# Weight halves at places inside their tiles that differ from load to load

## The chip, the cores and the metric

One Trainium2 chip, of which the kernel uses one core. The metric is the device time of one execution in microseconds (us), from the chip's own clock. The kernel is a single launch; weights come from the chip's memory inside the measured time.

## The reference, cut to what matters

Two transformer blocks of two layers each, in float32, on 512 positions of width 1024. The first block has, per layer, sliding-window attention, a causal depthwise convolution and latent attention side by side, gated and summed, then an MLP with a squared ReLU. The second block carries a second stream of 256 context positions through its first layer; that layer mixes differential attention with a recurrent (delta-rule) mixer, the next one a state-space scan with gated linear attention, and each ends in the same kind of MLP. What the change touches is the plain matrix product that stands in all of them:

```python
x = x + jnp.square(jax.nn.relu(h @ w_up[l])) @ w_down[l]          # first block, two layers
def _sq_relu_mlp(h, w1, w2):
    return jnp.square(jax.nn.relu(h @ w1)) @ w2                   # second block, two layers
```

## The kernel before, in words

Activations stand transposed in SBUF: 128 channels on the partitions, 512 positions (256 for the context stream) along the free axis. A product of a weight block of 1024x128 with the activations is eight steps of contraction, each on a 128x128 piece of the weights.

TensorE multiplies float32 here in a form that keeps fewer bits (fp32r), so every operand is split into a high part (the value cast to fp32r) and a low part (what the cast left out). `load_w` (from L211) does this for weights: SyncE brings a block of 128x1024 float32 into the tile `raw` (L222), ScalarE casts it into `whi` (L223) and VectorE writes the rest into `wlo` (L224). `split` (from L198) does the same for activations, into `hi` and `lo`. `mm3` (from L227) makes three matmuls of one step: `whi` with `hi` (L230), `whi` with `lo` (L231) and `wlo` with `hi` (L232). The weights are the stationary operand, loaded into the array once for each matmul (the rows of engine PEld), the activations the moving one. So one block costs 24 matmuls with 512 moving columns, and 24 more with 256 where the context stream runs along.

`weights(parts)` opens a pool for the weight tiles. Each of `raw`, `whi` and `wlo` has its buffers side by side, two of `raw` and `parts` of the other two, taken in turn by successive loads. `parts` is 2 nearly everywhere, 3 for a pool of the second block's first output projection (`out_proj`), and 4 for the last layer's MLP, which also does half of that layer's output projection. Every weight tile is 1024 float32 long, 4096 bytes on each partition, and its data begin at its first byte. Loads run ahead of their use: a load can start as soon as the buffer's last reader is done.

Where the tiles lie is decided when the program is built. Taken modulo 256 bytes (all weight buffers of one pool give the same number, since 4096 is a multiple of 256; so do the activations of one stage) the first bytes are, as the program is laid out:

| stage | moving tiles (`hi`, `lo`) | `whi`, `wlo` | difference |
|---|---|---|---|
| first block, all products (the two MLPs fill 400 to 870 us and 1210 to 1690 us) | 224 | 224 | 0 |
| second block, `out_proj`, output chunks 0 to 2 (weights from the pool of 3) | 64 | 64 | 0 |
| second block, `out_proj`, later chunks (weights from the pool of 2 on the other side) | 64 | 224 | 160 back, or 96 on |
| second block, first layer's MLP (to about 3115 us), both streams | 160 | 224 | 64 |
| second block, last layer's MLP (about 3580 to 3885 us) | 224 | 224 | 0 |

Other operands lie at places of their own. The convolution's taps (L638) read `u[:, j:j + T]` with j from 1 to 30, 4 bytes further at each tap. `conv` in `odd_features` writes `raw[:, 262:774]` (L1846), 1048 bytes into its tile. The weights of L1439 are a slice of a packed tile of constants that begins 40 bytes past a multiple of 64.

The order of the work is written out by hand: generators that `weave` advances in turn, one instruction stream per engine. The change moves nothing in it.

Of the kernel before, what the change touches and what calls it, by code (L numbers as in the profile page):

```python
# [20 lines left out]
P = 128  # L21
# [6 lines left out]
class Build:  # L28
    def __init__(self, tc, ctx, A, out, dbg=None):
        self.tc, self.nc, self.ctx, self.A, self.out = tc, tc.nc, ctx, A, out  # L30
        self.dbg = dbg or {}
        self.uid = 0
        self.phases, self.psp = [], []


# [174 lines left out]

    def load_w(self, src, kc, cols=P):  # L211
        nc = self.nc
        def t(tag, dt, bufs):
            w = self.wp.tile([P, 1024], dt, tag=tag, name=self.nm(tag), bufs=bufs)
            return w[:, :kc * cols].rearrange("p (k m) -> p k m", k=kc)
        raw, hi, lo = t("raw", F32, 2), t("whi", F32R, self.wparts), t("wlo", F32R, self.wparts)
        if isinstance(src, list):
            for i, one in enumerate(src):
                k = kc // len(src)
                nc.sync.dma_start(out=raw[:, i * k:i * k + k], in_=one.rearrange("p (k m) -> p k m", k=k))  # L220
        else:
            nc.sync.dma_start(out=raw, in_=src)  # L222
        nc.scalar.copy(out=hi, in_=raw)  # L223
        nc.vector.tensor_tensor(out=lo, in0=raw, in1=hi.bitcast(F32), op=ALU.subtract)  # L224
        return hi, lo
# [2288 lines left out]
```

## Time and profile before

| | us |
|---|---|
| median of two runs | 3913.18 |
| lowest and highest | 3912.67, 3913.69 |
| the profiled execution | 3924.51 |
| its span, first to last instruction | 3922.4 |
| mean granted TensorE clock in it | 0.969 of full speed |

The profile page gives each engine's busy time, the chain of work that ended last, and the costliest groups of instructions by line. PE is TensorE's matmuls, PEld its weight loads, DVE VectorE, ACT ScalarE, POOL GpSimd. Matmuls are pipelined: one begins before the one ahead of it has left the array, so the durations of a group add up to more than PE's busy time, and what a matmul costs in a stream is read from one start to the next.

### The profile page before, as it was taken

How to read it: one execution, taken by the hardware profiler on the slowest of the kernel's cores; microseconds unless marked ns; L12 is line 12 of the kernel's file. 1: busy time of each engine (PE TensorE's matmuls, PEld its weight loads, DVE VectorE, ACT ScalarE, POOL GpSimd, SP SyncE). 2: the span in 40 equal slices, each digit the busy share in tenths (PEclk: the TensorE clock that was granted, in tenths of full speed). 3: DMA queues.
4: the chain of work that ended last, by engine and by line, in shares of the span. 5: the costliest groups of instructions: out<-in, count | busy, mean ns of one | idle time of the engine just before them, and what ended most of it. 6: DMA issues, size and time to landing. Idle time of an engine off the chain costs nothing.

```text
span 3922.4 us, 54927 instructions
## 1 busy us (share of the span) xinstructions
PE 3765.1 (96%) x21506; PEld 2966.9 (76%) x21506; DVE 2398.5 (61%) x4178; ACT 1739.6 (44%) x3923; POOL 97.0 (2%) x204
## 2 busy tenths in 40 slices
PE   8999999999999999999998999899999999899998
PEld 5566888886667888778885666788888887678887
DVE  7587567665786566657646667554444574756444
ACT  4655343334553333335537788441222265533332
POOL 0000000000000000000001000000000000000000
PEclk9999999999999999999998989999999999879999
DMA  3132345542132355531110000212112212012232
GB/s 130 49 92 81 100 156 179 158 147 64 57 92 86 118 169 168 192 115 47 45 44 2 2 2 2 82 54 65 65 60 65 83 54 64 6 60 94 97 97 76
DMA packets 115699, 324.98 MB, mean 83 GB/s; under 512 B 12528, under 2 KB 34032, under 8 KB 115440
## 3 DMA queue, kind: packets, MB, share of 16 engines
q1 hardware_dynamic: 115440, 321.47, 25.6%
q8 instruction: 169, 2.77, 0.3%
q14 instruction: 90, 0.74, 0.1%
HBM read 307.27 MB, written 12.58 MB: 82 GB/s over the span
## 4 chain that ended last, share of the span: by engine, by line
PE 78%; issue 11%; ACT 6%; DVE 4%; POOL 1%; DMA 1%; SPq 0%; POOLq 0%; DVEq 0%; ACTq 0%
PE ps_g L230 20%; PE ps_g L232 20%; PE ps_g L231 20%; ACT B L1621 1%; PE ps_mm L1564 1%; PE ps_y L750 1%; PE ps_sc L740 1%; POOL r L308 1%; PE ps_y L825 1%; PE ps_z L1531 1%; PE ps_sc L796 1%; PE ps_g L2161 1%; PE ps_y L1236 1%; PE ps_sc L454 1%; DVE wlo L224 1%
## 5 line engine op out<-in xcount | busy, mean ns | idle before, releaser
L230 PE MATMUL ps_g<-hi,whi 128*128 128x512 f32 (+1 forms) x4464 | 1671.5, 375 | 21.2 <-ACT whi L223 13.6
L232 PE MATMUL ps_g<-hi,wlo 128*128 128x512 f32 (+1 forms) x4464 | 1655.7, 371 | 10.3 <-DVE wlo L224 10.2
L231 PE MATMUL ps_g<-lo,whi 128*128 128x512 f32 (+1 forms) x3744 | 1402.3, 375 | 2.3 <-DVE lo L954 1.8
L223 ACT CAST whi<-raw 128x1024 fp32r<-128x1024 f32 (+3 forms) x497 | 481.7, 970 | 1249.3 <-PE ps_g L231 1068.9
L230 PEld LDWEIGHTS ps_g<-hi,whi 128*128 128x128 f32 x4464 | 847.3, 190 | 190.3 <-ACT whi L223 23.7
L232 PEld LDWEIGHTS ps_g<-hi,wlo 128*128 128x128 f32 x4464 | 846.4, 190 | 167.1 <-DVE wlo L224 17.1
L231 PEld LDWEIGHTS ps_g<-lo,whi 128*128 128x128 f32 x3744 | 711.6, 190 | 135.1 <-issue 10.5
L224 DVE TENSOR_TENSOR wlo<-raw,whi 128x1024 fp32r<-128x1024 f32 (+3 forms) x497 | 557.2, 1122 | 165.2 <-ACT whi L223 159.4
L231 PE MATMUL ps_g<-x,whi 128*128 128x512 f32 (+1 forms) x720 | 252.4, 351 | 0.0
L1130 DVE SCALAR_TENSOR_TENSOR x<-ps_g,mod,x 128x512 f32<-128x512 f32 (+1 forms) x192 | 127.1, 662 | 203.3 <-PE ps_g L232 203.3
L879 DVE SCALAR_TENSOR_TENSOR macc<-mraw,cs,macc 128x1024 f32<-128x1024 f32 x140 | 175.7, 1279 | 7.8 <-DMA mraw<-in_mod_w 7.5
L638 DVE SCALAR_TENSOR_TENSOR cv<-u,taps,cv 128x512 f32<-128x512 f32 x240 | 177.2, 745 | 1.1
L1109 DVE TENSOR_SCALAR r<-ps_g 128x512 f32<-128x512 f32 x96 | 57.6, 602 | 184.1 <-PE ps_g L232 181.2
L231 PEld LDWEIGHTS ps_g<-x,whi 128*128 128x128 f32 x720 | 138.0, 192 | 16.4 <-issue 1.6
L589 DVE TENSOR_TENSOR x<-ps_g,x 128x512 f32<-128x512 f32 x64 | 44.1, 690 | 138.3 <-PE ps_g L232 138.2
L473 DVE TENSOR_TENSOR o<-ps_g,R 128x512 f32<-128x512 f32 x76 | 52.2, 690 | 114.6 <-PE ps_g L232 110.8
L1110 ACT ACTIVATE r<-r 128x512 f32<-128x512 f32 x96 | 53.5, 558 | 145.6 <-DVE r L1109 145.6
L308 POOL TENSOR_TENSOR r<-v,mhalf 128x4 f32<-128x4 f32 (+2 forms) x30 | 38.5, 1284 | 2801.4 <-DVE v L327 2135.6
L582 DVE SCALAR_TENSOR_TENSOR r<-ps_g,R 128x512 f32<-128x512 f32 x64 | 44.0, 688 | 81.3 <-PE ps_g L232 77.4
L204 DVE TENSOR_TENSOR lo<-r,hi 128x512 fp32r<-128x512 f32 x96 | 57.7, 601 | 40.7 <-ACT hi L203 40.7
L1621 ACT COPY B<-ps_lv 32x64 f32<-32x64 f32 x384 | 77.5, 202 | 6.3
L291 ACT ACTIVATE sq<-x 128x512 f32<-128x512 f32 (+1 forms) x91 | 49.1, 543 | 70.0 <-DVE x L1130 34.8
(509 smaller groups left out, 4581.1 us busy)
## 6 DMA issues: line engine op xcount, KB each, us to landing
raw<-in_l_mlp_w SPq DMA_DIRECT2D x128, 512.0 KB, 3.4
mraw<-in_mod_w SPq DMA_DIRECT2D x96, 512.0 KB, 4.4
raw<-in_w_in SPq DMA_DIRECT2D x82, 512.0 KB, 3.5
raw<-in_w_up SPq DMA_DIRECT2D x64, 512.0 KB, 3.5
raw<-in_w_down SPq DMA_DIRECT2D x64, 512.0 KB, 3.5
raw<-in_l_w_in SPq DMA_DIRECT2D x50, 512.0 KB, 3.5
raw<-in_w_branch SPq DMA_DIRECT2D x48, 256.0 KB, 2.9
bias<-biasD SPq DMA_DIRECT2D x16, 512.0 KB, 3.9
```

The costliest lines, as they stand in the source:

```text
L204: nc.vector.tensor_tensor(out=lo, in0=src, in1=hi.bitcast(F32), op=ALU.subtract)
L223: nc.scalar.copy(out=hi, in_=raw)
L224: nc.vector.tensor_tensor(out=lo, in0=raw, in1=hi.bitcast(F32), op=ALU.subtract)
L230: t.matmul(ps, w[0], x[0], start=start, stop=False)
L231: t.matmul(ps, w[0], x[1], start=False, stop=False)
L232: t.matmul(ps, w[1], x[0], start=False, stop=stop)
L308: self.nc.gpsimd.tensor_tensor(out=r, in0=v, in1=self.mhalf[:, :v.shape[1]], op=ALU.pow)
L638: nc.vector.scalar_tensor_tensor(out=y, in0=u[:, j:j + T], scalar=taps[:, c * 31 + j:c * 31 + j + 1], in1=y, op0=ALU.mult, op1=ALU.add)
L879: nc.vector.scalar_tensor_tensor(out=acc[s], in0=rw, scalar=self.cs[:, k, s:s + 1], in1=acc[s], op0=ALU.mult, op1=ALU.add)
L1109: nc.vector.tensor_scalar(out=t, in0=ps[s][:, :n], scalar1=0.0, scalar2=None, op0=ALU.max)
L1130: nc.vector.scalar_tensor_tensor(out=xx[c], in0=ps[:, :n], scalar=md[:, s, 5, c:c + 1], in1=xx[c], op0=ALU.mult, op1=ALU.add)
L1621: nc.scalar.copy(out=B[rows, :, j, :], in_=blocks(ps[rows, 0:64]))
```

## The change

`load_w` makes the tiles of `whi` and `wlo` longer by `pad` elements (16, and 128 where the pool has four parts), and lets their data begin at an offset that steps through sixteen values, one at each load: 0 to 15 elements (0 to 60 bytes, by 4), or 0 to 120 elements (0 to 480 bytes, by 32) in the last layer. The high and low parts of one load have the same offset. `raw` stays as it was. No instruction is added, removed or moved.

```diff
-        self.uid = 0
+        self.uid = self.nload = 0
...
     def load_w(self, src, kc, cols=P):
         nc = self.nc
+
+        self.nload += 1
+        pad = 128 if self.wparts == 4 else 16
+
         def t(tag, dt, bufs):
-            w = self.wp.tile([P, 1024], dt, tag=tag, name=self.nm(tag), bufs=bufs)
-            return w[:, :kc * cols].rearrange("p (k m) -> p k m", k=kc)
+            o = 0 if tag == "raw" else self.nload % 16 * (pad // 16)
+            w = self.wp.tile([P, 1024 + (0 if tag == "raw" else pad)], dt, tag=tag, name=self.nm(tag), bufs=bufs)
+            return w[:, o:o + kc * cols].rearrange("p (k m) -> p k m", k=kc)
         raw, hi, lo = t("raw", F32, 2), t("whi", F32R, self.wparts), t("wlo", F32R, self.wparts)
```

## Rows read from the trace of the kernel before

**Rows 1.** The page: busy time by engine, and the chain that ended last.
```profile
PE 3765.1 (96%) x21506; PEld 2966.9 (76%) x21506; DVE 2398.5 (61%) x4178; ACT 1739.6 (44%) x3923; POOL 97.0 (2%) x204
...
PE 78%; issue 11%; ACT 6%; DVE 4%; POOL 1%; DMA 1%; SPq 0%; POOLq 0%; DVEq 0%; ACTq 0%
```

**Rows 2.** Groups by line and shape: count, busy us, mean ns, idle before and releasers.
```profile
L230 PE MATMUL ps_g<-hi,whi 128*128 128x512 f32 x3432 | 1374.9, 401 | 18.8 <-ACT whi L223 11.2 <-ACT hi L206 6.9 <-ACT hi L953 0.6
...
L224 DVE TENSOR_TENSOR wlo<-raw,whi 128x1024 fp32r<-128x1024 f32 x417 | 509.8, 1223 | 164.8 <-ACT whi L223 158.9 <-PE ps_r L2073 0.7
L223 ACT CAST whi<-raw 128x1024 fp32r<-128x1024 f32 x417 | 438.2, 1051 | 1177.1 <-PE ps_g L231 1044.9 <-issue 109.1 <-DMA raw<-in_l_w_out 7.0
L230 PE MATMUL ps_g<-hi,whi 128*128 128x256 f32 x1016 | 290.3, 286 | 2.4 <-ACT whi L223 2.4
```

**Rows 3.** Four stretches, matmuls that read wlo alone (one in three): length, busy (count), clock.
```profile
400.00:870.00 470.00, 263.14 (x676) 1.00 0.47 150
...
1210.00:1690.00 480.00, 265.09 (x677) 0.99 0.46 149
...
2520.00:3115.00 595.00, 374.72 (x1108) 1.00 0.20 63
...
3580.00:3885.00 305.00, 174.61 (x449) 1.00 0.31 100
```

**Rows 4.** Timeline of PE, first block's MLP: start us, duration; the second is 24 later.
```profile
499.98 0.39 PE L230 MATMUL ps_g<-hi,whi 128*128 128x512 f32 x1
...
505.42 0.39 PE L230 MATMUL ps_g<-hi,whi 128*128 128x512 f32 x1
```

**Rows 5.** Timeline of PE, last layer's MLP: the second is 24 matmuls later.
```profile
3650.14 0.39 PE L230 MATMUL ps_g<-hi,whi 128*128 128x512 f32 x1
...
3655.58 0.39 PE L230 MATMUL ps_g<-hi,whi 128*128 128x512 f32 x1
```

**Rows 6.** Timeline of PE, out_proj, weights of the pool of 3: twelve matmuls apart.
```profile
2510.99 0.39 PE L232 MATMUL ps_g<-hi,wlo 128*128 128x512 f32 x1
...
2513.71 0.39 PE L232 MATMUL ps_g<-hi,wlo 128*128 128x512 f32 x1
```

**Rows 7.** Timeline of PE, out_proj, weights of the other pool: each 24 matmuls apart.
```profile
2529.23 0.28 PE L230 MATMUL ps_g<-hi,whi 128*128 128x256 f32 x1
...
2532.11 0.39 PE L230 MATMUL ps_g<-hi,whi 128*128 128x512 f32 x1
...
2537.71 0.28 PE L230 MATMUL ps_g<-hi,whi 128*128 128x256 f32 x1
```

**Rows 8.** Timeline of PE, second block's first MLP: each 24 matmuls apart.
```profile
2701.17 0.28 PE L230 MATMUL ps_g<-hi,whi 128*128 128x256 f32 x1
...
2704.00 0.39 PE L230 MATMUL ps_g<-hi,whi 128*128 128x512 f32 x1
...
2709.59 0.28 PE L230 MATMUL ps_g<-hi,whi 128*128 128x256 f32 x1
```

**Rows 9.** Timeline of PE after a break, first block: five matmuls, then three more.
```profile
256.05 0.39 PE L231 MATMUL ps_g<-lo,whi 128*128 128x512 f32 x1
...
257.20 0.39 PE L230 MATMUL ps_g<-hi,whi 128*128 128x512 f32 x1
...
257.88 0.39 PE L230 MATMUL ps_g<-hi,whi 128*128 128x512 f32 x1
```

**Rows 10.** Groups by line and shape: operands at odd places (all but L951).
```profile
L638 DVE SCALAR_TENSOR_TENSOR cv<-u,taps,cv 128x512 f32<-128x512 f32 x240 | 177.2, 745 | 1.1
...
L951 DVE SCALAR_TENSOR_TENSOR t<-x,gs,R 128x512 f32<-128x512 f32 x24 | 17.0, 746 | 4.5 <-ACT R L342 4.5
...
L1846 ACT COPY raw<-ps_g 128x512 f32<-128x512 f32 x8 | 4.7, 582 | 8.3 <-PE ps_g L232 8.3
...
L1439 PEld LDWEIGHTS ps_mm<-feat,cv 64*128 64x128 f32 x48 | 7.6, 185 | 5.0 <-issue 2.9 <-DVE S L1712 0.5 <-DVE Mh L1566 0.3
```

**Rows 11.** Timeline: a weight load and a copy of 128x512 at even places.
```profile
3500.30 0.19 PEld L230 LDWEIGHTS ps_r<-hi,whi 128*128 128x128 f32 x1
...
3511.26 0.59 ACT L342 COPY R<-ps_r 128x512 f32<-128x512 f32 x1 [8.09 <-PE ps_r L339]
```

## The prediction

> **What bounds the kernel now.** I read the page first: engine shares, then the chain. PE is busy for 96% of the span and stands for 78% of the chain that ended last, with 11% more in which PE mostly just issues; VectorE is at 61% and ScalarE at 44% [rows 1]. So this is a kernel bound by TensorE, and a change to the weights matters if it changes what a matmul costs, or if it makes ScalarE or VectorE late with a weight tile. The groups by line and shape say which matmuls count: each of the three lines of `mm3` has some 3432 with 512 moving columns and 1016 with 256, so about 10,300 wide ones and 3,050 narrow ones in all, and they hardly ever wait for a weight tile: 11.2 us in total for `whi` ahead of the wide ones of L230 [rows 2].
>
> What one of them costs is read in the timeline, from start to start, because the durations overlap. In the first block's MLP 24 wide matmuls take 505.42 - 499.98 = 5.44 us, 226.7 ns each [rows 4]. In the last layer's MLP it is 3655.58 - 3650.14 = 5.44 us, the same [rows 5]. In the second block's first MLP it is 2709.59 - 2704.00 = 5.59 us, 232.9 ns [rows 8], though the shape, the engine and the code are the same and the granted clock is 1.00 in this stretch as in the others [rows 3]. That difference is what the prediction is about.
>
> The table of places gives a reason. Where the spacing is 226.7 ns, the moving tiles and the weight tiles begin at the same byte modulo 256; where it is 233 ns they don't. The best evidence is `out_proj`, since there the moving tiles are the same ones throughout and only the pool of the weights changes. With weights at the same place modulo 256, twelve wide matmuls take 2513.71 - 2510.99 = 2.72 us, 226.7 ns each [rows 6]; with weights from the other pool, 160 bytes off, 24 take 2537.71 - 2532.11 = 5.60 us, 233.3 ns each [rows 7]. So the place of the weights relative to the moving operand is worth 6.6 ns of 226.7 on a wide matmul. For narrow ones it is little and of either sign: 2532.11 - 2529.23 = 2.88 us for 24, or 120.0 ns, at a difference of 160 [rows 7], and 2704.00 - 2701.17 = 2.83 us, or 117.9 ns, at a difference of 64 [rows 8].
>
> One more thing is seen where PE was held up: after a break the wide matmuls start at 230 ns (five from 256.05 to 257.20) and come to 226.7 ns only then (three from 257.20 to 257.88) [rows 9]. The low spacing is a rhythm that a run of matmuls falls into, and that only equal places let it keep.
>
> **The change part by part.** *The longer tiles.* 1040 elements are 4160 bytes, 64 more than a multiple of 256; so in a pool of two, the second buffer of `whi` and of `wlo` lies 64 bytes further, modulo 256, than the first. In the last layer 1152 elements are 4608 bytes, a multiple of 256, and all four buffers keep one place. The pools begin lower by a multiple of 256, so the first buffer's base stays where it was. The number of buffers is the same, no wait is added, and no transfer is moved.
>
> *The offsets.* In the pools of two and three, a load now begins 0 to 60 bytes past its buffer's base, so 0 to 124 bytes past the place of the moving tiles where both were equal. Only one load in sixteen, the one with offset 0, can still be at the same place, and only if it falls on the first buffer. In the last layer the offset goes through the sixteen multiples of 32 up to 480, and two of them (0 and 256) are equal modulo 256.
>
> *What a wide matmul then costs.* The trace has spacings for differences of 0, 64 and 160 bytes, and none for a difference that is no multiple of 32. Both nonzero ones give about 233 ns, so for a load that loses its equal place I take 233.3 - 226.7 = 6.6 ns more [rows 4, 7]. As for bounds: going from narrow to wide adds 226.7 - 120.0 = 106.7 ns for 256 columns [rows 4, 7], so the columns of a wide matmul cost 213.4 ns and 13.3 ns are a part that does not grow with them. The lower end is that this part goes, 13.3 ns less per matmul; the upper end, by the same measure, that it doubles, 13.3 ns more. I take the 6.6 from the nearest rows.
>
> *How many.* The matmuls that read `wlo` are one in three: 676, 677 and 449 in the two first MLPs and the last one [rows 3], so 2028 + 2031 + 1347 matmuls, all wide, in stretches that PE fills without a break at 226.7 ns. The first MLP of the second block has 3 x 1108 = 3324, half of them wide: 1662 at 233 ns already. The remaining wide ones, 10,296 - 5,406 - 1,662 = 3,228, stand between other work, where breaks restart the rhythm [rows 9]; I take a third of them, 1,076, as having reached it (an estimate between none and all). With 4-byte steps: (2028 + 2031 + 1076) x 15/16 x 6.6 ns = 31.8 us. In the last layer: 1347 x 14/16 x 6.6 ns = 7.8 us. In the second block's first MLP the difference was 64 and becomes 64 to 124 or 128 to 188: never equal, so 0. The narrow ones outside that MLP, some 1,390, may gain the 2.1 ns between 120.0 and 117.9 where they had an equal place; I take off 1 us.
>
> *The writers.* ScalarE now writes `whi`, and VectorE reads `whi` and writes `wlo`, at odd places. The nearest rows show no price: the convolution's taps, which read 4 bytes further each time, take 745 ns, and the same operation on even places 746 ns; a ScalarE copy to an odd place takes 582 ns, and one to an even place 590 ns [rows 10, 11]. A weight load at an odd place took 185 ns, one at an even place 190 ns [rows 10, 11]. A VectorE write at such a place is not among them. I take 0; the cover is the wait that ScalarE has in hand before its casts, 1044.9 us in total for buffers to come free [rows 2]. If both operations took half as long again, 1.05 and 1.22 us would become 1.6 and 1.8 us per load, still far under the 5.4 us of its 24 matmuls; only the first loads of a stage would show it, under 1 us each.
>
> *The sum.* 31.8 + 7.8 - 1 = 38.6 us, all on PE, and in stretches where PE is the chain, so it reaches the end. Against the profiled execution's own 3924.5 us that is 3963 us; the median of the runs is 11.3 us below that execution, and 3913.2 + 38.6 = 3952 us.
>
> A page of the Trainium skill says otherwise. "TensorE: Matmul & The Clock Gate", in its section "Step-by-step: what each phase is for", has PE read its moving operand and the next weights through two independent ports of SBUF, so that loading weights takes no read bandwidth from the running matmul. By that the place of the weights could not matter, and the kernel would stay at 3913 us. The trace does not agree in `out_proj`, where 226.7 ns became 233.3 ns with the weights' pool alone [rows 6, 7].
>
> **The rivals.** *Nothing happens.* The rhythm may depend on something that goes with those stages and not on the place itself, or differences under 32 bytes may count as none while the rest evens out. For it: only three differences are in the trace, and narrow matmuls hardly care. Against it: `out_proj`. Its time is 3913 us, or some 3930 us if half of the loads keep the low spacing.
>
> *Faster: the varied places break up what costs the 13.3 ns.* If equal places are themselves a standing collision of the weights' reads with the moving ones, and odd steps avoid half of it, then wide matmuls come to about 220 ns: 6.6 ns less for 5,406 + 1,076 (43 us), 13.3 ns less for the 1,662 (22 us), and 6.6 ns less for 3,048 narrow ones (20 us): 85 us, or 3828 us. It decides from the point at which spacings at odd offsets fall under 226.7 ns. For it: 13.3 ns stand in every matmul, whatever its width. Against it: of three places the equal one is the best.
>
> *Worse: odd starts cost more than unequal ones.* If a weight piece that starts inside a line of the memory makes the fixed part double, wide matmuls come to 240 ns: 13.3 ns more for some 6,480 (86 us), 6.6 for 1,662 (11 us), and up to 13.3 for the narrow ones (40 us): 137 us, 4050 us. For it: no row has a 4-byte start in this kind of matmul. Against it: the 185 ns of the odd weight load [rows 10].
>
> **How the numbers follow.** The forecast, 3952 us, gets 0.63, and its own range is 3930 to 3985 us (no locked matmul outside the MLPs gives 3945; all of them 3965; both with some play in the 6.6 ns). Nothing happens: 0.13. Faster: 0.12. Worse: 0.12. The range of 3890 to 4005 us leaves out most of the last two. Two per cent, about what a measurement of this kernel can tell from no change, is 78 us: the forecast and the first rival lie inside, the faster case straddles the lower bound, and the worse case lies mostly beyond the upper one. That gives 0.07 for faster, 0.80 for within, 0.13 for slower.
>
> **What would show it.** In the profile after, the timeline of the first block's MLPs should show wide matmuls at about 233 ns in nearly all loads, changing from load to load with a period of sixteen, and the windows of the two MLPs should be longer by about 13 us each (2028 x 15/16 x 6.6 ns = 12.5 us). The last layer should show two loads of every sixteen at 226.7 ns. The second block's first MLP should keep its length. L223 and L224 should keep 1051 and 1223 ns. I am wrong if wide matmuls in the first MLPs stay at 226.7 ns or fall below, if they pass 238 ns, or if the lost time stands ahead of PE as waits for L223 or L224.

## The result, and the profile after

The changed kernel takes 3953.35 us, the median of two runs (3948.09 and 3958.60), against 3913.18 us: a ratio of 1.0102, with a 95% interval of 1.0077 to 1.0126, that is 40 us slower, between 30 and 49. The forecast was 3952 us. The profiled execution took 3958.6 us at a mean granted clock of 0.970 of full speed; the one of before took 3924.5 us at 0.969. So the two profiles are 34.1 us apart and the clock is not the reason.

The page shows the same picture as before [rows 1]: busy time by engine, then the chain that ended last.

```profile
PE 3801.8 (96%) x21506; PEld 2969.3 (75%) x21506; DVE 2401.5 (61%) x4178; ACT 1740.7 (44%) x3923; POOL 98.1 (2%) x204
...
PE 78%; issue 11%; ACT 6%; DVE 4%; POOL 1%; DMA 0%; POOLq 0%; DVEq 0%; SPq 0%; ACTq 0%
```

Only PE moved: 3801.8 - 3765.1 = 36.7 us more, with the same 21,506 matmuls. VectorE and ScalarE are within 3 us. The chain has nearly the same shares. A kernel that waits more would show it in "issue" or in another engine's share; this one does the same work more slowly on PE.

The groups by line and shape (count, busy us, mean ns of one, idle before and releasers). The lines of `load_w` and `mm3` stand five further down than before:

```profile
L235 PE MATMUL ps_g<-hi,whi 128*128 128x512 f32 x3432 | 1384.4, 403 | 18.4 <-ACT whi L228 10.9 <-ACT hi L206 6.6 <-ACT hi L958 0.6
...
L229 DVE TENSOR_TENSOR wlo<-raw,whi 128x1024 fp32r<-128x1024 f32 x417 | 510.5, 1225 | 165.7 <-ACT whi L228 160.1 <-PE ps_r L2078 0.8
L228 ACT CAST whi<-raw 128x1024 fp32r<-128x1024 f32 x417 | 437.2, 1049 | 1212.6 <-PE ps_g L236 1078.9 <-issue 114.4 <-DMA raw<-in_l_w_out 6.9
```

The two writers keep their durations (1049 ns against 1051, 1225 against 1223 [rows 2]), and PE waits no longer for a high part than it did (10.9 us in total against 11.2). ScalarE waits longer for buffers (1078.9 us against 1044.9), because PE gives them back later. The mean of a matmul in the groups rises from 401 to 403 ns, which tells almost nothing: the durations overlap, so the cost has to be read from start to start.

How many matmuls that read `wlo` fit into the stretch of the first MLP (length, busy, count, clock) says it more plainly:

```profile
400.00:870.00 470.00, 260.83 (x661) 1.00 0.46 147
```

661 instead of 676 in the same 470 us [rows 3], at a granted clock of 1.00 both times: 2.2% fewer. The timeline of PE (start us, duration) shows why, at four marks in that stretch; the second row of each pair is 24 matmuls after the first.

```profile
500.01 0.40 PE L235 MATMUL ps_g<-hi,whi 128*128 128x512 f32 x1
...
505.57 0.40 PE L235 MATMUL ps_g<-hi,whi 128*128 128x512 f32 x1
...
522.31 0.39 PE L235 MATMUL ps_g<-hi,whi 128*128 128x512 f32 x1
...
527.81 0.39 PE L235 MATMUL ps_g<-hi,whi 128*128 128x512 f32 x1
```

The first load takes 5.56 us, 231.7 ns a matmul; its high part lies 60 bytes past the place of the moving tiles modulo 256, its low part 188. The other takes 5.50 us, 229.2 ns, with the parts 12 and 140 bytes past. Before, 24 took 5.44 us, 226.7 ns [rows 4]. In the second block's first MLP the rows are these (24 wide ones, then 24 narrow ones):

```profile
2727.45 0.39 PE L235 MATMUL ps_g<-hi,whi 128*128 128x512 f32 x1
...
2733.03 0.28 PE L235 MATMUL ps_g<-hi,whi 128*128 128x256 f32 x1
...
2735.87 0.40 PE L235 MATMUL ps_g<-hi,whi 128*128 128x512 f32 x1
```

232.5 ns and 118.3 ns: as before [rows 8]. And in the last layer (offsets, taken modulo 256: 0, then 32, and further on 192 bytes; 24 matmuls each):

```profile
3705.68 0.39 PE L235 MATMUL ps_g<-hi,whi 128*128 128x512 f32 x1
...
3711.13 0.39 PE L235 MATMUL ps_g<-hi,whi 128*128 128x512 f32 x1
...
3716.72 0.40 PE L235 MATMUL ps_g<-hi,whi 128*128 128x512 f32 x1
...
3739.13 0.40 PE L235 MATMUL ps_g<-hi,whi 128*128 128x512 f32 x1
...
3744.64 0.40 PE L235 MATMUL ps_g<-hi,whi 128*128 128x512 f32 x1
```

At offset 0 they take 5.45 us (227.1 ns), at 32 bytes 5.59 us (232.9), at 192 bytes 5.51 us (229.6).

One load of the second MLP stands out, the one with offset 44 bytes (24 matmuls):

```profile
1479.94 0.42 PE L235 MATMUL ps_g<-hi,whi 128*128 128x512 f32 x1
...
1485.81 0.39 PE L235 MATMUL ps_g<-hi,whi 128*128 128x512 f32 x1
```

It takes 5.87 us, 244.6 ns a matmul, and the next one with this offset, sixteen loads on, takes as long (1570.92 to 1576.79 us). A load of the first MLP with the same offset in the same buffer took 5.59 us (752.30 to 757.89). The loads of the first MLP with offset 28 differ too: 5.44 us at 638.24 us, but 5.60 us at 730.02. So the place alone doesn't say what a load with a 4-byte offset takes; what else does, no run here shows.

Since no instruction moved, each matmul of `load_w`'s weights has its twin in the other trace, and the starts of the twins say where the 34 us came in. Of the 34.0 us between the first and the last such matmul, the two first MLPs give 10.3 and 11.5, the last one 7.6, and the second block's first MLP gives back 2.1. The remaining 6.7 us are the sum over all the other stages, which moved by several us either way.

### The profile page after: what moved, and what is told of

It is laid out like the page before. It is cut to its first block, busy times and chain, and to the rows that moved or that the text cites. A ratio compares the mean times of both kernels' runs of the same rounds, so it can differ in the third digit from the quotient of the medians.

```text
span 3956.5 us, 54926 instructions
## 1 busy us (share of the span) xinstructions
PE 3801.8 (96%) x21506; PEld 2969.3 (75%) x21506; DVE 2401.5 (61%) x4178; ACT 1740.7 (44%) x3923; POOL 98.1 (2%) x204
## 4 chain that ended last, share of the span: by engine, by line
PE 78%; issue 11%; ACT 6%; DVE 4%; POOL 1%; DMA 0%; POOLq 0%; DVEq 0%; SPq 0%; ACTq 0%
PE ps_g L235 20%; PE ps_g L237 20%; PE ps_g L236 20%; ACT B L1626 1%; PE ps_mm L1569 1%; PE ps_y L755 1%; PE ps_sc L745 1%; POOL r L313 1%; PE ps_y L830 1%; PE ps_sc L801 1%; PE ps_g L2166 1%; PE ps_y L1241 1%; PE ps_z L1536 1%; PE ps_sc L459 1%; PE ps_lv L1616 1%
## 5 line engine op out<-in xcount | busy, mean ns | idle before, releaser
L237 PE MATMUL ps_g<-hi,wlo 128*128 128x512 f32 (+1 forms) x4464 | 1666.8, 374 | 10.3 <-DVE wlo L229 10.2
```

The lines of the kernel that those rows point to most:

```text
L237: t.matmul(ps, w[1], x[0], start=False, stop=stop)
```

## The experiments

Three theories stood against each other. A, the prediction's: what counts is where the weights begin modulo 256 bytes, measured from where the moving tiles begin, however they come to lie there. V: it counts that the place differs from load to load. O: starts that are no multiple of 32 bytes count by themselves. All these kernels compute the whole reference. The kernel before, run beside them, had a median of 3912.49 us (24 runs, first four experiments) and 3914.08 us (23 runs, last four).

The table gives, for each profile, how much longer a stage took than in the profile of before, in us from twin start to twin start, with the ratio of the whole kernel's time in the last row. The number of `load_w` matmuls in the stage stands in brackets.

| stage | after | e1 | e2 | e3 | e4 | e5 | e6 | e7 | e8 |
|---|---|---|---|---|---|---|---|---|---|
| first MLP (2000 wide) | +10.3 | +9.6 | 0.0 | +6.7 | 0.0 | 0.0 | +10.3 | +12.9 | 0.0 |
| second MLP (2000 wide) | +11.5 | +7.8 | -0.6 | +1.9 | -2.2 | -2.2 | +12.7 | +12.0 | -2.2 |
| second block's first MLP (3100, half of them narrow) | -2.1 | -1.5 | -1.5 | -4.1 | -4.7 | -5.9 | -2.1 | -0.2 | -9.8 |
| last MLP (1432 wide) | +7.6 | 0.0 | 0.0 | +3.2 | 0.0 | +7.6 | 0.0 | +9.5 | 0.0 |
| ratio of the times | 1.0102 | 1.0059 | 1.0005 | 1.0039 | 0.9980 | 1.0015 | 1.0071 | 1.0105 | 0.9964 |

The rows hold breaks (here, spacings over 260 ns) as well as what lies between them. The second MLP is 2.2 us shorter in e4, e5 and e8, which don't touch it, because the profile of before has 2.2 us more of breaks there; so the values of that row can be low by up to as much.

**e1: the longer tiles without the offsets.**

```diff
-            o = 0 if tag == "raw" else self.nload % 16 * (pad // 16)
+            o = 0 if tag == "raw" else 0
```

> The longer tiles alone, with every offset 0. All places are multiples of 32 bytes; in the pools of two, the second buffer and the low parts are moved by 64, 128 and 192 bytes modulo 256, so 4032 of the 10,656 wide matmuls stand at equal places instead of 8560; the last layer stays equal. Theory A (a wide matmul runs at 226.7 ns only where the weights and the moving operand begin at the same byte modulo 256, at about 233 ns elsewhere): 20 to 28 us slower than before, nearly all that the change cost outside the last layer, since a block whose low part is unequal doesn't settle even where its high part is equal. Rival O (starts that are no multiple of 32 bytes cost it): 0 to 3 us slower.

Measured: 3934.45 us, 1.0059 [1.0040, 1.0078], some 22 us slower. So about half of the change's cost is there with every datum at its tile's first byte. The timeline in the first MLP, rows 24 matmuls apart:

```profile
501.93 0.39 PE L235 MATMUL ps_g<-hi,whi 128*128 128x512 f32 x1
...
507.48 0.40 PE L235 MATMUL ps_g<-hi,whi 128*128 128x512 f32 x1
...
513.05 0.39 PE L235 MATMUL ps_g<-hi,whi 128*128 128x512 f32 x1
```

5.55 us, then 5.57 us: 231.3 and 232.1 ns. In the second of the two loads the high part begins at the moving tiles' place, and it is no faster. Its low part does not begin there: the buffers of `wlo` stand behind the two of `whi`, 2 x 4160 = 8320 bytes on, which is 128 modulo 256. One matmul in three at another place is enough to lose the low spacing for all three, and that is what the prediction had overlooked. In the last layer, where the tiles stayed a multiple of 256 bytes long, nothing moved.

**e2: offsets of 0 and 256 bytes in turn, in the last layer alone** (from the kernel before).

```diff
+        self.nload += 1
+        pad = 64 if self.wparts == 4 else 0
...
+            o = 0 if tag == "raw" else self.nload % 2 * pad
+            w = self.wp.tile([P, 1024 + (0 if tag == "raw" else pad)], dt, tag=tag, name=self.nm(tag), bufs=bufs)
```

> The last layer alone: tiles 256 bytes longer, and the offset alternates from load to load between 0 and 256 bytes, so that the place varies but is equal modulo 256 at each load. Theory A: no change in the last layer, its 24 matmuls of a block at 226.7 ns each; within 3 us of before in all. Rival V (that the place differs from load to load is what breaks the rhythm): about 6 us slower, as the last layer was with the change.

Measured: 3912.52 us, 1.0005 [0.9995, 1.0016]: no change. The timeline of the last layer, 24 matmuls apart:

```profile
3706.60 0.39 PE L234 MATMUL ps_g<-hi,whi 128*128 128x512 f32 x1
...
3712.04 0.39 PE L234 MATMUL ps_g<-hi,whi 128*128 128x512 f32 x1
```

5.44 us, 226.7 ns. A place that changes from load to load costs nothing as long as it changes by 256 bytes. This speaks against V.

**e3: all weights at one other place, 64 bytes lower.** A tile of 64 bytes, which nothing uses, is added to each pool at its first load.

```diff
+        if self.wend is not self.wp:
+            self.wend = self.wp
+            self.wp.tile([P, 16], F32, tag="end", name=self.nm("end"), bufs=1)
```

> Every weight tile 64 bytes lower, by a tile of 64 bytes at the end of each pool; nothing varies from load to load and nothing is at an odd place. Theory A: the wide matmuls at equal places go from 8560 to 2104 (those of the second block's first MLP become equal). The two first MLPs gain about 12 us each, the last one 9 us, the second block's first MLP loses 8 to 10 us; in all 25 to 38 us slower. Rivals V and O: no change, within 3 us, and no change in any MLP.

Measured: 3926.0 us, 1.0039 [1.0025, 1.0053], some 14 us slower: the right sign, but about half of what was expected. The timeline, first in the first MLP (24 matmuls), then in the second block's first MLP (24 wide, 24 narrow), where the weights have now come to the moving tiles' place:

```profile
505.35 0.39 PE L234 MATMUL ps_g<-hi,whi 128*128 128x512 f32 x1
...
510.84 0.39 PE L234 MATMUL ps_g<-hi,whi 128*128 128x512 f32 x1
...
2691.59 0.40 PE L234 MATMUL ps_g<-hi,whi 128*128 128x512 f32 x1
...
2697.06 0.28 PE L234 MATMUL ps_g<-hi,whi 128*128 128x256 f32 x1
...
2699.93 0.40 PE L234 MATMUL ps_g<-hi,whi 128*128 128x512 f32 x1
```

At 64 bytes short of the moving tiles, 192 past modulo 256, a wide matmul takes 5.49 us / 24 = 228.8 ns, not 233. So "unequal" is not one price. In the other MLP the wide ones came down to 5.47 / 24 = 227.9 ns, from 232.9 [rows 8], and the narrow ones went up to 2.87 / 24 = 119.6 ns, from 117.9.

The last layer of the changed kernel holds the whole scale, since its loads pass through all multiples of 32. The mean spacing of wide matmuls there, over 66 to 88 of them at each offset:

| bytes past the moving tiles | 0 | 32 | 64 | 96 | 128 | 160 | 192 | 224 |
|---|---|---|---|---|---|---|---|---|
| ns | 226.7 | 233.2 | 233.3 | 234.1 | 233.3 | 233.5 | 229.0 | 233.3 |
| 256 further, ns | 226.7 | 233.2 | 233.3 | 234.1 | 233.4 | 233.5 | 229.0 | 233.2 |

The two rows agree within 0.1 ns: the period is 256 bytes. Six of the seven unequal places cost 6.5 to 7.4 ns, and the one at 192 costs 2.3.

**e7: the same with a tile of 192 bytes**, so that the weights lie 192 bytes lower, 64 past the moving tiles modulo 256, where the scale says 233.3 ns.

```diff
-            self.wp.tile([P, 16], F32, tag="end", name=self.nm("end"), bufs=1)
+            self.wp.tile([P, 48], F32, tag="end", name=self.nm("end"), bufs=1)
```

> Every weight tile 192 bytes lower, which is 64 bytes past the equal place where the kernel before is equal (the earlier run put them 64 bytes short of it). Nothing varies from load to load. Theory A with a price that depends on the difference (64 past: 6.6 ns per wide matmul, 64 short: 2.6 ns): the first block's and the last layer's wide matmuls at 233 ns, 36 to 46 us slower than before. Rival: any unequal place costs what 64 short did, and the rest of the change's cost comes from variation or odd starts: 12 to 18 us slower.

Measured: 3954.49 us, 1.0105 [1.0087, 1.0123]: 40 us slower, as much as the change itself, with no offset, no odd start and no variation. The timeline in the first MLP (24 matmuls):

```profile
503.43 0.39 PE L234 MATMUL ps_g<-hi,whi 128*128 128x512 f32 x1
...
509.03 0.39 PE L234 MATMUL ps_g<-hi,whi 128*128 128x512 f32 x1
```

5.60 / 24 = 233.3 ns, and in the window of that MLP there are four matmuls fewer still than after the change:

```profile
400.00:870.00 470.00, 259.76 (x657) 1.00 0.43 147
```

This shows A: place alone, held constant, gives a cost as large as the whole change's, and neither V nor O has an explanation for it. What it doesn't settle is whether 4-byte starts add something of their own in the matmuls: no run holds such a place constant, and the load at 244.6 ns has one.

**e5 and e6: the change in the last layer alone, and everywhere else.**

```diff
# e5
+        pad = 128 if self.wparts == 4 else 0
+            o = 0 if tag == "raw" else self.nload % 16 * 8 if self.wparts == 4 else 0
# e6
+        pad = 0 if self.wparts == 4 else 16
+            o = 0 if tag == "raw" else 0 if self.wparts == 4 else self.nload % 16
```

> The change in the last layer alone (its longer tiles and the offsets by 32 bytes); the other pools as before. Theory A: the last layer's MLP is 6 to 8 us longer and no other stage moves; 5 to 9 us slower in all. In each sixteen loads the two at offsets 0 and 256 run at 226.7 ns. A rival by which the change's cost comes from the pool's size or from later loads would show waits ahead of PE there; A shows none.

> The change everywhere but in the last layer (longer tiles and offsets by 4 bytes). Theory A: 28 to 36 us slower than before, what the whole change cost less the last layer's part, and 5 to 13 us more than the longer tiles alone cost, since those still left some places equal. If starts at 4 bytes have a price of their own, it stands in this difference and the spacings rise above 235 ns on the mean; A expects 231 to 234 ns.

Measured: e5 3920.43 us, 1.0015 [1.0002, 1.0028], 6.3 us slower; e6 3942.26 us, 1.0071 [1.0055, 1.0087], 28.2 us slower. Together 34.5 us, within the change's own interval of 30 to 49. In the profiles the last MLP of e5 and the first MLP of e6 are longer by exactly what they are after the whole change, 7.6 and 10.3 us, so the parts don't disturb each other there. (The second MLP of e6 is 12.7 us longer, against 11.5.) In e5's last MLP no spacing is over 260 ns, so no wait stands ahead of PE. In e6 the mean spacing, breaks left out, is 232.0 ns in the first MLP and 233.1 in the second, between the 231 and 234 that A expected. Against e1 (22 us), the 4-byte offsets add about 6 us; that they do it by moving loads off the few cheaper places is argued and not shown, and the loads with offset 44 are part of it.

The timeline of e5 holds something else. The second block's first MLP, which e5 doesn't touch (24 wide, 24 narrow), and then two loads of the last layer (offsets 224 and 0 modulo 256):

```profile
2697.61 0.39 PE L235 MATMUL ps_g<-hi,whi 128*128 128x512 f32 x1
...
2703.21 0.28 PE L235 MATMUL ps_g<-hi,whi 128*128 128x256 f32 x1
...
2705.93 0.39 PE L235 MATMUL ps_g<-hi,whi 128*128 128x512 f32 x1
...
3706.35 0.40 PE L235 MATMUL ps_g<-hi,whi 128*128 128x512 f32 x1
...
3711.94 0.39 PE L235 MATMUL ps_g<-hi,whi 128*128 128x512 f32 x1
...
3717.39 0.39 PE L235 MATMUL ps_g<-hi,whi 128*128 128x512 f32 x1
```

In the last layer 5.59 us and 5.45 us, as in the changed kernel. But the narrow ones take 2.72 / 24 = 113.3 ns here, against 117.9 ns in the profile of before at the same places [rows 8]. That made this stage 5.9 us shorter, and it is the second reason, beside the scale, why a place alone doesn't fix a spacing.

**e4: the other way round, the moving tiles brought to the weights.** In the kernel before, tiles that nothing uses shift the activations of `out_proj` by 160 bytes and those of the second block's first layer's MLP by 64 (and one of 192 bytes on the right side, in the phase ahead of them), so that they begin where the weights do.

```diff
+                    self.tl([P, 48], F32, "gap")
...
-        with self.phase(h=16), self.banks(g=4, z=2, mm=2):
+        with self.phase(h=16, gap=1), self.banks(g=4, z=2, mm=2):
+            self.tl([P, 40], F32, "gap")
...
+            if both:
+                self.tl([P, 16], F32, "gap")
```

> Weights as before; the moving tiles of the second block's first layer are moved, by gaps of 160, 64 and 192 bytes in three of its pools, to the byte modulo 256 at which its weights begin. Wide matmuls at equal places go from 8560 to 10,632 of 10,656; 1656 narrow ones become equal too. Theory A: the wide ones of that layer's MLP come down from 233 to 226.7 ns (10 us) and 2 us elsewhere, the narrow ones rise from 117.8 to about 119.7 ns (3 us): 6 to 12 us faster than before. Rivals V and O: no change, within 3 us.

Measured: 3903.42 us, 0.9980 [0.9971, 0.9990], 9 us faster, as expected in total but not in its parts. The timeline of the second block's first MLP: 24 narrow ones, and further on twice six wide ones.

```profile
2690.76 0.28 PE L230 MATMUL ps_g<-hi,whi 128*128 128x256 f32 x1
...
2693.64 0.40 PE L230 MATMUL ps_g<-hi,whi 128*128 128x512 f32 x1
...
2697.82 0.40 PE L230 MATMUL ps_g<-hi,whi 128*128 128x512 f32 x1
...
2699.20 0.39 PE L230 MATMUL ps_g<-hi,whi 128*128 128x512 f32 x1
...
2700.56 0.28 PE L230 MATMUL ps_g<-hi,whi 128*128 128x256 f32 x1
```

The narrow ones take 2.88 / 24 = 120.0 ns and the wide ones 2.74 / 12 = 228.3 ns. The wide ones lost some 4.6 ns each, less than the 6 that equal places are worth, because they begin anew at 230 ns (1.38 us for the first six) after a run of narrow ones, as they do after a break [rows 9], and come to 226.7 (1.36 us for the next six) only then; and the narrow ones became 2.1 ns slower. The MLP is 4.7 us shorter in the profile. The rest of the 9 us lies in other stages and isn't settled.

**e8: e4, with the narrow stream's tiles left 64 bytes short.** Three more such tiles in the MLP's phase put the moving tiles of the context stream back to a difference of 64, where narrow ones were quicker, while those of the wide stream stay equal.

```diff
+                self.tl([P, 48], F32, "gap2")
...
+            if both:
+                self.tl([P, 16], F32, "gap3")
...
+                        if s and e == 0 and not us[s]:
+                            self.tl([P, 48], F32, "gap4")
```

> The run with equal places, and in the second block's first MLP the moving tiles of the narrow matmuls back at their difference of 64 bytes, by three more gaps in that pool; the wide ones stay equal. Theory A: wide ones there at 226.7 to 228 ns, narrow ones at 117.8 instead of 119.8 ns, so 3 us faster than the run with equal places and 9 to 15 us faster than before. If a narrow run at an unequal place costs the wide run behind it more settling, the gain is under 1 us.

Measured: 3899.18 us, 0.9964 [0.9952, 0.9977], 15 us faster than the kernel before. It beats both kernels. The timeline (24 wide, 24 narrow):

```profile
2696.66 0.39 PE L230 MATMUL ps_g<-hi,whi 128*128 128x512 f32 x1
...
2702.10 0.28 PE L230 MATMUL ps_g<-hi,whi 128*128 128x256 f32 x1
...
2704.93 0.39 PE L230 MATMUL ps_g<-hi,whi 128*128 128x512 f32 x1
```

5.44 / 24 = 226.7 ns and 2.83 / 24 = 117.9 ns. The wide ones now hold their lowest spacing, although narrow runs stand between them as in e4. With 9.8 us, this MLP gives most of the gain.

## Why the prediction was right

The total was right, 38.6 us forecast and 40 measured, and so was the cause. That the two lie within 2 us of each other is partly luck: the measured interval is 30 to 49 us, and in the two profiles, where the terms can be told apart, they add up to 34.0 us. By its steps:

*What bounds the kernel.* Right. The time came as PE's own spacing: PE busy 36.7 us longer, no new wait, the same chain.

*The place of the weights relative to the moving operand is what a wide matmul's spacing hangs on.* Right, and now shown by edits and not only by a comparison of stages: a constant shift costs 40 us (e7), a shift of 256 bytes nothing (e2), and bringing the places together where they differed gains 9 to 15 us (e4, e8). That "only equal places" let the low spacing be kept was too strong: the load with offset 28 at 638.24 us, with its parts 28 and 156 bytes past, ran at 227 ns. The Trainium skill's rule of two independent read ports ("TensorE: Matmul & The Clock Gate", "Step-by-step: what each phase is for") names no effect of the place; e7's 233.3 ns against 226.7 ns shows one. Whether it arises at these ports, no run here shows.

*The longer tiles.* This is the step that failed, without harm to the sum. The prediction moved the second buffer of each tag by 64 bytes and let the load with offset 0 keep its equal place in the first. It left out that `wlo`'s buffers stand behind both of `whi`'s, 128 bytes further modulo 256. So no load in the pools of two has all three matmuls of a step at the moving tiles' place, and the tiles' length alone costs half of the change (e1).

*The price per matmul.* 6.6 ns at 15 loads of 16 was expected, 6.2 ns on average. Breaks left out, the spacing rose from 226.8 to 232.0 ns in the first MLP, by 5.2 ns, and from 226.9 to 233.1 in the second, by 6.2 ns. "Both nonzero ones give about 233 ns, so 6.6" took two places for all: the scale has a cheaper one, 192 bytes, and the loads with 4-byte offsets ran anywhere from 227 to 244.6 ns. This term was sized at 12.5 us for each MLP and measured 10.3 and 11.5 (the latter with 0.7 us less of breaks in the profile after). The overlooked `wlo` and the lower price worked against each other.

*The last layer.* 7.8 us forecast for 1347 matmuls, 8.3 for the 1432 that the stage has; 7.6 measured, twice. Two offsets of sixteen at 226.7 ns, as said, and two more at 229.0.

*The second block's first MLP.* 0 forecast, -2.1 us measured. e2, which doesn't touch that stage, shows -1.5, so most of it is play between executions.

*All other stages.* 1,076 matmuls, 6.7 - 1 = 5.7 us, were forecast; the profiles give +6.7. The count was short: `load_w` has 10,656 wide matmuls, not 10,296, since its groups under other tile names were left out. Given how far these stages move from one execution to the next, that agreement is no proof of the third that was taken.

*The writers.* Right: 0 forecast, 1049 and 1225 ns against 1051 and 1223. Odd starts have no price of their own in the cast or the subtraction; for the weight loads the mean stayed at 190 ns.

*The rivals.* "Nothing happens" fell with the ratio's interval. "Faster" fell with the spacings: no load of the first MLPs or the last one is under 226.7 ns. Its premise, 13.3 ns that stand in every matmul whatever the width, fell with e5, where narrow ones ran at 113.3 ns, half of 226.7. "Worse" fell as a rule, since the mean is 232.0 and 233.1 ns in the first MLPs and not 240; but the load with offset 44 in the second of them does run at 244.6 ns. The prediction had named spacings over 238 ns there as a sign that it is wrong, and for this one load in sixteen it was.

## What to carry to other kernels

Where a stream of matmuls like these (fp32r, 512 columns) loads its weights anew for each, compare where the weights and the moving tiles begin, modulo 256 bytes, before comparing anything else; equal places were worth 3% of each wide matmul here, at no instruction. A few spare bytes at the end of a tile are not free: they shift every buffer behind them, the other tags' too, so pad by a multiple of 256 bytes or not at all. And look for stages that run the same shape at two spacings in one trace: they name the price and the cure.

## What the runs showed that I had not expected

The price is periodic in 256 bytes but not symmetric: 64 bytes past costs 6.6 ns, 64 short 2.3. What in the chip makes 256 bytes the period, and why 192 is half spared, no run here shows.

The place doesn't fix the spacing alone, as the loads with offsets 28 and 44 show for wide matmuls. Narrow matmuls at a difference of 64 bytes ran at 117.9 ns in the profile of before and in e8, and at 113.3 in e5's through the whole stage. Twenty-four of them are 0.11 us apart, and the stage 4 to 6 us; that this makes part of the 20 us by which runs of one kernel differ is only argued.

Wide and narrow matmuls seem to want different places: wide ones ran quickest at equal ones, narrow ones at 64 past rather than at equal places (117.9 ns against 119.6 to 120.0). And what the narrow runs do carries over: wide ones between narrow ones at 120.0 ns start anew at 230 ns (e4), between narrow ones at 117.9 they keep 226.7 (e8).
